# A planned one-core encoder layer: listed times of loads and small steps, and where a gate's tile is loaded

## The chip, the cores and the metric

The kernel runs on one core of one Trainium2 chip. The metric is the device time of one execution in microseconds, as the median of several; a shorter time is better. The engines are named as the profile names them: PE (TensorE), ACT (ScalarE), DVE (VectorE), POOL (GpSimd) and SP (SyncE, whose queue issues nearly all DMAs).

## The reference

One layer over a sequence of 2048 tokens of width 1024, in float32. Two mixers read the same normalised input: banded attention over chunks of 64 tokens (8 heads) and an mLSTM, a matrix memory carried from chunk to chunk (4 heads). Their gated sum is projected and added, and a feed-forward part of width 4096 follows.

```python
xn = rms_norm(x, mix_norm_g)
aq, ak, av, mq, mk, mv, mo, ipre, fpre, ga, gm = split(xn @ w_in)
att = chunk_band_attention(aq, ak, av, rel_bias)
hm = mlstm_chunkwise(*silu(conv(mq, mk)), mv, ipre + b_igate, fpre + b_fgate)
mlstm_out = sigmoid(mo) * rms_norm(hm, mh_norm_g)          # per head; the output gate
y = sigmoid(ga) * (att @ w_att_proj) + sigmoid(gm) * (mlstm_out @ w_mlstm_proj)
x = x + y @ w_out
x = x + square(relu(rms_norm(x, ffn_norm_g) @ w_up)) @ w_down
return rms_norm(x, final_norm_g)
```

## The kernel before

The 2048 tokens are four blocks of 512 (b = 0 to 3), handled as two halves of two. Every dense product is computed with operands split into two parts of reduced precision, so that each product is three matmuls of 512 columns (`mm3`, `quad`, `product`, `down`), and the large products are cut by Strassen's scheme into seven sub-products, m = 0 to 6. What such a sub-product needs on the activations' side (a sum of blocks, split in two) is an operand; a weight tile is loaded into `wraw` and split into `wsp` (ACT L483, DVE L485).

The first pass over the input projection serves blocks 0 and 1 (`quad`), the second pass serves blocks 2 and 3 (`in_far`), in three batches of sub-products, (0, 3, 1), (2, 4) and (5, 6). The second pass's operands are computed early and kept in device memory as `xu`. `take_batch` loads them into a ring of 16 tiles: for each m and k it waits for the tile to be kept and for a free ring slot, and spawns `take_u1`, which loads (L2055) and splits the tile (a cast on ACT, L1061, and a subtraction on DVE, L1066). Four loads serve one m.

The mixers of blocks 0 and 1 run beside the second pass, those of blocks 2 and 3 beside the first half's downward product. They consist of many small steps. For attention, `scores` multiplies (L1289), finds maxima (DVE, L1295), takes exponentials (ACT, L1302) and normalises on ACT or DVE (L1309, L1307), `turn` transposes (L1321) and splits (L1324, L1326), and `weigh` multiplies by the values (L1214), which were loaded from `vspill` (L1093). For the mLSTM, `gates_rest` computes a block's gate sums in some sixty steps on tiles of 16 columns, and `rec_head` computes one head of one block: it waits for its loads (`load_rec`), weighs the scores in tile `w`, multiplies `w` by the values for each of four chunks (L1564) with the carried state (L1568, L1572), collects the outputs (`rec_out`), normalises them in eight steps on tiles of 4 columns, transposes them (L1603), and multiplies them by the output gate (L1605), which it loads from `mfar` into a tile of the pool `temp` (L1599). One head is worked on at a time (`rec_room`).

At the start `norm_in(b)` sums the squares of blocks 0 and 1 (L977), takes the inverse root on POOL (L981, L985), and `rows_far` spreads it over the partitions with PE (L1020).

The order of the work comes from a planner, `Flow`. Each part is a generator; it yields the engine that it needs and how long it takes there in ns (and, as a third number, how long its result takes to land after that), or it waits for an event or a free tile. The planner keeps a clock for each engine and always lists the request that could start first. The instructions come out in that order, and a scheduler behind it lists each engine's own queue, in which ACT's and DVE's instructions may be pulled ahead by up to 6 and 10 us of planner's time. A load is planned like this:

```python
yield "sp", 800, 2000            # SP for 800 ns; landed 2000 ns later
self.nc.sync.dma_start(r[:, 1].bitcast(F32), src)
yield from self.split(r[:, 1].bitcast(F32), r)
```

So the numbers in the yields move instructions within the queues; they do not change what the chip does with one. Each engine works its queue off in order, and an instruction whose input is late holds what stands behind it.

Of the kernel before, what the change touches and what calls it, by code (L numbers as in the profile page):

```python
# [36 lines left out]
MH = 4  # L37
# [65 lines left out]
class Flow:  # L103
# [11 lines left out]
               dve=dict(pe=220.0, act=130.0, dve=130.0, pool=155.0), pool=dict(pe=290.0, act=130.0, dve=60.0),  # L115
# [119 lines left out]
def dve_ns(n):  # L235
    return 70 + 1.042 * n
# [12 lines left out]
class Layer:  # L249
# [710 lines left out]
    def norm_in(self, b):  # L960
        fl, nc = self.fl, self.nc
        B = self.blk[b]
        r, ev = self.rin[b], [Event() for _ in range(KT)]
        (slot,) = yield "get", self.sc, 1
        tot = slot[0]
        B["xg"] = yield "get", self.rpool, KT
        fl.set(B["xg_ev"])
        if b == 1:
            yield "wait", self.w_sent
        for k in range(KT):  # L970
            (x,) = yield "get", self.ctx, 1
            fl.spawn(self.square_in(b, k, x, tot, ev), b)
        yield "wait", ev
        (bk,) = yield "get", self.banks, 1
        yield "pe~", 900
        for t in range(NT):
            nc.tensor.matmul(bk[:, 2 * t:2 * t + 2], tot[:, t * P:(t + 1) * P], self.ones,  # L977
                             start=True, stop=True)
        fl.put(self.sc, slot)
        yield "dve", 75  # L980
        nc.vector.tensor_scalar(r, bk[:, :2 * NT].rearrange("p (t a) -> p t a", a=2)[:, :, 0], 1.0 / D, EPS,  # L981
                                op0=ALU.mult, op1=ALU.add)
        fl.put(self.banks, bk)
        yield "pool", 3600
        nc.gpsimd.tensor_tensor(r, r, self.half, op=ALU.pow)  # L985
        fl.set(self.ev_r[b])
    def stats_far(self):
# [396 lines left out]
    def gates_rest(self, b, bk):  # L1384
# [10 lines left out]
        yield "dve", 85  # L1395
        V.tensor_scalar(d, e, 2.0, None, op0=ALU.add)
        yield "dve", 85
        V.reciprocal(d, d)
        yield "dve", 85
        V.tensor_mul(s, e, d)  # L1400
        yield "dve", 85
        V.tensor_mul(s2, s, s)
        yield "dve", 85
        V.tensor_scalar(p, s2, 1.0 / 15, None, op0=ALU.mult)
        for m in (13, 11, 9, 7, 5, 3):
            yield "dve", 85
            V.scalar_tensor_tensor(p, p, 1.0 / m, s2, op0=ALU.add, op1=ALU.mult)
        yield "dve", 85
        V.scalar_tensor_tensor(p, p, 1.0, s, op0=ALU.add, op1=ALU.mult)
        yield "dve", 85  # L1410
        V.tensor_scalar(v4("lf"), fg, 0.0, None, op0=ALU.min)
        yield "dve", 85
        V.scalar_tensor_tensor(sm["lf"], p, -2.0, sm["lf"], op0=ALU.mult, op1=ALU.add)
        yield "pe~", 300
        nc.tensor.matmul(bk[:, 0:16], self.tri, sm["lf"], start=True, stop=True)
        nc.tensor.matmul(bk[:, 16:32], self.ones[:, 0:1].to_broadcast([P, P]), sm["lf"], start=True, stop=True)
        yield "dve", 85
        V.tensor_copy(sm["bc"], bk[:, 0:16])
        yield "dve", 85
        V.tensor_copy(sm["bl"], bk[:, 16:32])  # L1420
        yield "dve", 85
# [4 lines left out]
        yield "dve", 85  # L1426
        V.tensor_copy(a[:, 64:], bk[:16, 128:256])
        sh = 1
        while sh < P:
# [9 lines left out]
        yield "dve", 85  # L1439
        V.tensor_copy(sm["um"], bk[:, 272:288])  # L1440
        ms, ml, bl = self.ms, v4("ml"), v4("bl")
        if b > 0:
            yield "dve", 85
            V.tensor_copy(ms[:, 0], ms[:, NT])
        for c in range(NT):
            yield "dve", 85
            V.tensor_tensor(ml[:, c], ms[:, c], um[:, c], op=ALU.max)
            yield "dve", 85
            V.tensor_add(ms[:, c + 1], ml[:, c], bl[:, c])
        msf = ms.rearrange("p a b -> p (a b)")[:, :16]  # L1450
        yield "dve", 85
        V.tensor_tensor(sm["mt"], msf, bk[:, 256:272], op=ALU.max)
        ex = self.ex
        yield "dve", 85
        V.scalar_tensor_tensor(ex[:, 0], sm["mt"], -1.0, sm["bc"], op0=ALU.mult, op1=ALU.subtract)
        yield "dve", 85
        V.tensor_sub(ex[:, 1], msf, sm["mt"])
        yield "dve", 85
        V.tensor_sub(ex[:, 2], sm["u"], sm["ml"])
        yield "dve", 85  # L1460
        V.tensor_sub(ex[:, 3], msf, sm["ml"])
        yield "act", 150
        nc.scalar.activation(ex, ex, AF.Exp)
        yield "dve", 85
        V.tensor_scalar(ex[:, 1], ex[:, 1], 0.5, None, op0=ALU.mult)
        yield "dve", 85
# [55 lines left out]
    def rec_head(self, b, h, r):  # L1522
# [53 lines left out]
        yield "dve", 85  # L1576
        V.scalar_tensor_tensor(hs[:, 0], den, -1.0, den, op0=ALU.mult, op1=ALU.max)
        yield "dve", 85
        V.tensor_tensor(hs[:, 0], hs[:, 0], exh, op=ALU.max)
        yield "dve", 85  # L1580
        V.reciprocal(hs[:, 0], hs[:, 0])
        yield "dve", 85
        V.tensor_mul(hs[:, 1], hs[:, 0], hs[:, 0])
        yield "dve", 85
        V.tensor_mul(hs[:, 1], hs[:, 1], hs[:, 2])
        yield "dve", 85
# [3 lines left out]
        yield "dve", 85  # L1590
        V.tensor_mul(hs[:, 0], hs[:, 0], hs[:, 1])
        yield "dve", dve_ns(512)
        V.tensor_mul(ndv[:, :, :128], ndv[:, :, :128],
                     hs[:, 0].rearrange("p (c o) -> p c o", o=1).to_broadcast([P, NT, P]))
        fl.put(self.hs, hs)
        (og,) = yield "get", self.temp, 1
        yield "wait", [self.m_ev[b, 2 * MH + h]]
        yield "sp", 800, 2000
        nc.sync.dma_start(og[:, :512], self.mfar[b].ap()[2 * MH + h])  # L1599
        (bk,) = yield "get", self.banks, 1  # L1600
        yield "pe~", 107 * NT
        for c in range(NT):
            nc.tensor.transpose(bk[:, c * P:(c + 1) * P], ndv[:, c, :128], self.ident)  # L1603
        yield "dve", dve_ns(512)
        V.tensor_mul(kt[:, :512], bk, og[:, :512])  # L1605
# [10 lines left out]
        fl.put(self.rpool, r)  # L1616
        fl.put(self.rec_room, 0)
        fl.set(B["rec_ev"][h])

    def rec_out(self, n, bk, nd, hs, c, ev, old):  # L1620
        fl, nc = self.fl, self.nc
# [428 lines left out]
        yield "wait", aev[ORDER[-1], 3]  # L2050
        fl.put(self.rpool, *(yield "get", ring, N_RING[s]))

    def take_u1(self, src, r, ev):
        yield "sp", 800, 2000
        self.nc.sync.dma_start(r[:, 1].bitcast(F32), src)  # L2055
        yield from self.split(r[:, 1].bitcast(F32), r)
        self.fl.set(ev)
# [279 lines left out]
    def build(self):  # L2337
# [37 lines left out]
        for b in range(NB):  # L2375
            self.blk.append(dict(
                xg=[], xg_ev=Event(), xn=E(KT), x2=E(KT), kq_all=Event(), begun=Event(), opened=Event(), how={}, mix_got=Event(), head_done=E(AH), gates=Event(), ctx={},
                qk_ev=E(2 * MH), mix=[None] * 8, mix_ev=E(8), mixed=E(8), mix_left=[4] * 4 + [1] * 4, rec_ev=E(MH),
                mid=Event(), vo={}, vn={}, vp_ev=E(4), mvh_ev=E(MH), row_ev=E(MH), rows=Event(), gf=Event(), heads_left=[2] * 4))
        fl.spawn(self.setup(), 0)  # L2380
        fl.spawn(self.norm_in(0), 0)
# [103 lines left out]
```

## Time and profile before

| | us |
|---|---|
| median of 3 runs (lowest to highest) | 2751.83 (2751.77 to 2754.45) |
| the profiled execution | 2750.82 |
| its span, first to last instruction | 2749.0 |
| PE busy | 2725.4 |
| DVE busy | 2085.9 |
| ACT busy | 1527.8 |
| POOL busy | 44.0 |
| DMA, mean rate | 245 GB/s |

The profile comes from one execution. Busy times add up the instructions of an engine; PE's matmuls overlap one another, so PE counts as busy where they follow each other without a hole. The granted clock of PE is 0.998 of full speed over the whole span.

### The profile page before, as it was taken

To read this page: it belongs to the slowest core of one execution; us is meant where nothing else is said; L and a number is where in the kernel's file an instruction comes from. 1 tells how busy PE (TensorE), PEld (TensorE's weight loads), DVE (VectorE), ACT (ScalarE), POOL (GpSimd) and SP (SyncE) were. 2 spreads that over 40 slices of the span, in tenths; PEclk is the share of its full clock that TensorE was granted. 3 is DMA by queue.
4 is the path that set the end of the run, shared out by engine and by line. 5 is a ranking of instruction groups with operands and counts; after the bars stand their busy time and mean duration, and the time that the engine had idled before them with its cause. 6 is when DMAs were issued, how large, how long until landed. Compare 5 with 4: busy or idle time off the path is not lost.

```text
span 2749.0 us, 38064 instructions
## 1 busy us (share of the span) xinstructions
PE 2725.4 (99%) x12840; PEld 2263.1 (82%) x12840; DVE 2085.9 (76%) x3686; ACT 1527.8 (56%) x2635; POOL 44.0 (2%) x76
## 2 busy tenths in 40 slices
PE   9999999999999999999999999999999999999998
PEld 7878888788888888888888888888888888888887
DVE  7868776888775778897668899888788665667675
ACT  6545446666652434566556766656345565564443
POOL 0000000000000000000000000000000000000000
PEclk9999999999999999999999999999999999999999
DMA  8877678778777898767668777786774454578763
GB/s 286 288 257 262 240 264 280 254 238 269 251 256 254 299 319 289 250 212 262 247 235 296 254 239 227 240 254 203 279 239 164 154 202 158 187 272 283 273 233 126
DMA packets 330840, 673.05 MB, mean 245 GB/s; under 512 B 36772, under 2 KB 66852, under 8 KB 330644
## 3 DMA queue, kind: packets, MB, share of 16 engines
q1 hardware_dynamic: 330500, 670.60, 72.5%
q8 instruction: 101, 1.65, 0.2%
q14 instruction: 95, 0.78, 0.1%
q10 hardware_dynamic: 144, 0.01, 0.0%
HBM read 458.27 MB, written 212.21 MB: 244 GB/s over the span
## 4 chain that ended last, share of the span: by engine, by line
PE 86%; DVE 6%; issue 3%; DMA 2%; ACT 2%; POOL 0%; SPq 0%; POOLq 0%; ACTq 0%; DVEq 0%
PE bank L613 36%; PE bank L644 12%; PE bank L545 9%; PE bank L544 9%; PE bank L546 9%; PE bank L649 2%; PE bank L1289 2%; PE bank L1214 2%; PE bank L1321 2%; DVE wsp L485 1%; DVE r L1066 1%; PE bank L1372 1%; PE bank L1564 0%; DVE sc L1295 0%; DVE ctx L1717 0%
## 5 line engine op out<-in xcount | busy, mean ns | idle before, releaser
L613 PE MATMUL bank<-r,wsp 128*128 128x512 f32 x4872 | 1111.1, 390 | 2.6 <-DVE r L1066 0.7
L613 PEld LDWEIGHTS bank<-r,wsp 128*128 128x128 f32 x4872 | 912.2, 188 | 197.0 <-DVE ctx L1750 2.0
L483 ACT CAST wsp<-wraw 128x1024 fp32r<-128x1024 f32 x439 | 461.1, 1050 | 460.5 <-PE bank L613 182.6
L485 DVE TENSOR_TENSOR wsp<-wraw,wsp 128x1024 fp32r<-128x1024 f32 x439 | 536.4, 1222 | 231.9 <-ACT wsp L483 228.7
L544 PE MATMUL bank<-r,wsp 128*128 128x512 f32 x1152 | 455.0, 395 | 0.3 <-DVE scs L1295 0.3
L546 PE MATMUL bank<-r,wsp 128*128 128x512 f32 x1152 | 450.2, 391 | 0.0
L545 PE MATMUL bank<-r,wsp 128*128 128x512 f32 x1152 | 450.1, 391 | 0.0
L644 PE MATMUL bank<-r,wsp 128*128 128x512 f32 x1512 | 370.1, 394 | 0.7 <-ACT r L1324 0.6
L644 PEld LDWEIGHTS bank<-r,wsp 128*128 128x128 f32 x1512 | 279.4, 188 | 56.5 <-ACT r L1324 0.8
L546 PEld LDWEIGHTS bank<-r,wsp 128*128 128x128 f32 x1152 | 216.3, 188 | 45.5
L544 PEld LDWEIGHTS bank<-r,wsp 128*128 128x128 f32 x1152 | 216.5, 188 | 41.0 <-DVE scs L1295 0.7
L545 PEld LDWEIGHTS bank<-r,wsp 128*128 128x128 f32 x1152 | 216.7, 188 | 40.4
L1066 DVE TENSOR_TENSOR r<-r 128x512 fp32r<-128x512 f32 x273 | 181.9, 686 | 70.5 <-ACT r L1061 69.2
L1061 ACT CAST r<-r 128x512 fp32r<-128x512 f32 x273 | 165.1, 620 | 126.1 <-DMA r<-u 101.3
L1750 DVE TENSOR_TENSOR ctx<-bank,ctx 128x512 f32<-128x512 f32 x150 | 102.7, 686 | 64.1 <-PE bank L613 63.0
L502 DVE TENSOR_TENSOR wraw<-wraw,wraw 128x1024 f32<-128x1024 f32 x112 | 136.3, 1218 | 1.9 <-DMA wsum<-wraw 0.7
L1302 ACT ACTIVATE sc<-sc,scs 128x640 f32<-128x640 f32 (+4 forms) x128 | 97.3, 761 | 54.0 <-DVE scs L1295 53.4
L1742 ACT COPY ctx<-bank 128x512 f32<-128x512 f32 x150 | 87.2, 581 | 52.4 <-PE bank L613 51.5
L2071 ACT ACTIVATE ctx<-ctx 128x512 f32<-128x512 f32 x96 | 60.5, 630 | 99.2 <-DVE ctx L1750 99.1
L1326 DVE TENSOR_TENSOR r<-bank,r 128x512 fp32r<-128x512 f32 (+1 forms) x168 | 96.4, 594 | 8.8 <-ACT r L1324 8.0
L1214 PE MATMUL bank<-r,r 128*128 128x512 f32 x336 | 95.8, 367 | 3.3 <-DVE ctx L1626 2.9
L1324 ACT CAST r<-bank 128x512 fp32r<-128x512 f32 (+1 forms) x168 | 80.8, 514 | 27.7 <-PE bank L1321 27.2
(246 smaller groups left out, 2975.3 us busy)
## 6 DMA issues: line engine op xcount, KB each, us to landing
wraw<-in_wf SPq DMA_DIRECT2D x196, 512.0 KB, 4.2
wraw<-wsum SPq DMA_DIRECT2D x112, 512.0 KB, 5.1
r<-u SPq DMA_DIRECT2D x224, 256.0 KB, 4.8
u<-ctx SPq DMA_DIRECT2D x128, 256.0 KB, 2.8
u<-tmp SPq DMA_DIRECT2D x96, 256.0 KB, 2.1
wraw<-in_w SPq DMA_DIRECT2D x47, 512.0 KB, 3.8
ctx<-in_wf SPq DMA_DIRECT2D x88, 256.0 KB, 4.2
wsum<-ctx SPq DMA_DIRECT2D x88, 256.0 KB, 2.9
```

What stands on the lines that cost most here:

```text
L483: nc.scalar.copy(w[:, 0], raw)
L485: nc.vector.tensor_sub(w[:, 1], raw, w[:, 0].bitcast(F32))
L502: V.tensor_sub(dst, x, y)
L544: mm(ps, lh, rh, start=first, stop=False)
L545: mm(ps, lh, rl, start=False, stop=False)
L546: mm(ps, ll, rh, start=False, stop=last)
L613: mm(ps, wv[:, x, k, n], a[:, y], start=new and k == 0 and x == y == 0, stop=k == 3 and x == 1, skip_group_check=True)
L644: mm(ps, wv[:, x, k, n], a[:, y], start=start and x == y == 0, stop=stop and x == 1, skip_group_check=True)
L1061: self.nc.scalar.copy(dst[:, 0], src)
L1066: self.nc.vector.tensor_sub(dst[:, 1], src, dst[:, 0].bitcast(F32))
L1214: nc.tensor.matmul(bkv[:, :, c0:c0 + w], st, sl[:, :, o:o + w], start=n == 0, stop=n == total - 1)
L1750: nc.vector.tensor_add(t[:, o:o + 512], ps, t[:, o:o + 512])
```

## The change

Four edits, all in what the planner is told or where a tile is kept.

1. `take_batch` tells the planner that a load of the second pass's operands lands 4500 ns after its issue; 2000 before. The other users of `take_u1` keep 2000.
2. `norm_in` tells it that the inverse root on POOL lands 3000 ns after its 3600 in the case b = 0; for b = 1 nothing is added.
3. In `rec_head` the output gate's tile is loaded into `w`, the tile of the weighted scores, which nobody reads after the last chunk's product. The load is a generator of its own, `load_gate`, spawned when the last chunk's product is listed, before the wait for the outputs. Before, a `temp` tile was taken and the load was listed after the normalisation. The multiplication waits for the new event `og_ev`.
4. The small DVE steps of `gates_rest` and `rec_head` are planned with 150 ns each instead of 85.

```diff
@@ take_batch
-                fl.spawn(self.take_u1(self.xud.ap()[m, k], r, aev[m][k]), 0)
+                fl.spawn(self.take_u1(self.xud.ap()[m, k], r, aev[m][k], 4500), 0)
@@ norm_in
-        yield "pool", 3600
+        yield "pool", 3600, 0 if b else 3000
@@ gates_rest, 25 places (some in loops), and rec_head, 7 places
-        yield "dve", 85
+        yield "dve", 150
...
@@ rec_head
+        fl.spawn(self.load_gate(b, h, w), 1)
         yield "wait", nev
...
         fl.put(self.hs, hs)
-        (og,) = yield "get", self.temp, 1
-        yield "wait", [self.m_ev[b, 2 * MH + h]]
-        yield "sp", 800, 2000
-        nc.sync.dma_start(og[:, :512], self.mfar[b].ap()[2 * MH + h])
         (bk,) = yield "get", self.banks, 1
         yield "pe~", 107 * NT
         for c in range(NT):
             nc.tensor.transpose(bk[:, c * P:(c + 1) * P], ndv[:, c, :128], self.ident)
+        yield "wait", [B["og_ev"][h]]
         yield "dve", dve_ns(512)
-        V.tensor_mul(kt[:, :512], bk, og[:, :512])
+        V.tensor_mul(kt[:, :512], bk, w[:, :512])
         fl.put(self.banks, bk)
-        fl.put(self.temp, og)
...
+    def load_gate(self, b, h, w):
+        yield "wait", [self.m_ev[b, 2 * MH + h]]
+        yield "sp", 800, 2000
+        self.nc.sync.dma_start(w[:, :512], self.mfar[b].ap()[2 * MH + h])
+        self.fl.set(self.blk[b]["og_ev"][h])
@@ take_u1
-    def take_u1(self, src, r, ev):
-        yield "sp", 800, 2000
+    def take_u1(self, src, r, ev, landing=2000):
+        yield "sp", 800, landing
```

More of the change, by code (lines that the diff above doesn't have):

```diff
@@ L1394, in gates_rest @@
         e, d, s, s2, p = (sm[n] for n in ("e", "d", "s", "s2", "p"))
-        yield "dve", 85
+        yield "dve", 150
         V.tensor_scalar(d, e, 2.0, None, op0=ALU.add)
-        yield "dve", 85
+        yield "dve", 150
         V.reciprocal(d, d)
-        yield "dve", 85
+        yield "dve", 150
         V.tensor_mul(s, e, d)
-        yield "dve", 85
+        yield "dve", 150
         V.tensor_mul(s2, s, s)
-        yield "dve", 85
+        yield "dve", 150
         V.tensor_scalar(p, s2, 1.0 / 15, None, op0=ALU.mult)
         for m in (13, 11, 9, 7, 5, 3):
-            yield "dve", 85
+            yield "dve", 150
             V.scalar_tensor_tensor(p, p, 1.0 / m, s2, op0=ALU.add, op1=ALU.mult)
-        yield "dve", 85
+        yield "dve", 150
         V.scalar_tensor_tensor(p, p, 1.0, s, op0=ALU.add, op1=ALU.mult)
-        yield "dve", 85
+        yield "dve", 150
         V.tensor_scalar(v4("lf"), fg, 0.0, None, op0=ALU.min)
-        yield "dve", 85
+        yield "dve", 150
         V.scalar_tensor_tensor(sm["lf"], p, -2.0, sm["lf"], op0=ALU.mult, op1=ALU.add)
@@ L1416, in gates_rest @@
         nc.tensor.matmul(bk[:, 16:32], self.ones[:, 0:1].to_broadcast([P, P]), sm["lf"], start=True, stop=True)
-        yield "dve", 85
+        yield "dve", 150
         V.tensor_copy(sm["bc"], bk[:, 0:16])
-        yield "dve", 85
+        yield "dve", 150
         V.tensor_copy(sm["bl"], bk[:, 16:32])
-        yield "dve", 85
+        yield "dve", 150
         V.tensor_sub(v4("u"), ig, v4("bc"))
@@ L1442, in gates_rest @@
         if b > 0:
-            yield "dve", 85
+            yield "dve", 150
             V.tensor_copy(ms[:, 0], ms[:, NT])
         for c in range(NT):
-            yield "dve", 85
+            yield "dve", 150
             V.tensor_tensor(ml[:, c], ms[:, c], um[:, c], op=ALU.max)
-            yield "dve", 85
+            yield "dve", 150
             V.tensor_add(ms[:, c + 1], ml[:, c], bl[:, c])
         msf = ms.rearrange("p a b -> p (a b)")[:, :16]
-        yield "dve", 85
+        yield "dve", 150
         V.tensor_tensor(sm["mt"], msf, bk[:, 256:272], op=ALU.max)
         ex = self.ex
-        yield "dve", 85
+        yield "dve", 150
         V.scalar_tensor_tensor(ex[:, 0], sm["mt"], -1.0, sm["bc"], op0=ALU.mult, op1=ALU.subtract)
-        yield "dve", 85
+        yield "dve", 150
         V.tensor_sub(ex[:, 1], msf, sm["mt"])
-        yield "dve", 85
+        yield "dve", 150
         V.tensor_sub(ex[:, 2], sm["u"], sm["ml"])
-        yield "dve", 85
+        yield "dve", 150
         V.tensor_sub(ex[:, 3], msf, sm["ml"])
@@ L1575, in rec_head @@
         exh = ex[:, 0].rearrange("p (c m) -> p c m", c=NT)[:, :, h]
-        yield "dve", 85
+        yield "dve", 150
         V.scalar_tensor_tensor(hs[:, 0], den, -1.0, den, op0=ALU.mult, op1=ALU.max)
-        yield "dve", 85
+        yield "dve", 150
         V.tensor_tensor(hs[:, 0], hs[:, 0], exh, op=ALU.max)
-        yield "dve", 85
+        yield "dve", 150
         V.reciprocal(hs[:, 0], hs[:, 0])
-        yield "dve", 85
+        yield "dve", 150
         V.tensor_mul(hs[:, 1], hs[:, 0], hs[:, 0])
-        yield "dve", 85
+        yield "dve", 150
         V.tensor_mul(hs[:, 1], hs[:, 1], hs[:, 2])
-        yield "dve", 85
+        yield "dve", 150
         V.tensor_scalar(hs[:, 1], hs[:, 1], 1.0 / P, EPS, op0=ALU.mult, op1=ALU.add)
```

12 lines of the change are left out of this document (6 added, 6 removed).

## The prediction, made before the changed kernel was run

> **What bounds the kernel now.** I read the page's first part, then the windows by stage, then PE's waits, then the timeline at the longest wait.
>
> ```profile
> span 2749.0 us, 38064 instructions
> ...
> PE 2725.4 (99%) x12840; PEld 2263.1 (82%) x12840; DVE 2085.9 (76%) x3686; ACT 1527.8 (56%) x2635; POOL 44.0 (2%) x76
> ```
>
> PE is busy in 2725.4 of 2749.0 us, so only what is not matmul work can be won: 23.6 us of idle time and what slow stretches of PE hide. The windows say where it lies (span and PE busy are the first two numbers, the granted clock is the third from the end).
>
> ```profile
> 450.00:750.00 300.00, 293.91 (x1603) 248.35 (x1602) 239.78 (x664) 201.05 (x468) 13.01 (x25) 1.00 0.82 259
> ...
> 1450.00:1950.00 500.00, 496.99 (x2610) 419.49 (x2609) 430.08 (x1031) 329.75 (x675) 17.86 (x32) 1.00 0.78 248
> 1950.00:2700.00 750.00, 748.97 (x3319) 620.02 (x3318) 528.58 (x686) 390.46 (x569) 2.94 (x2) 1.00 0.63 219
> 2700.00:2749.00 49.00, 40.45 (x211) 34.26 (x210) 20.44 (x29) 13.67 (x20) 2.01 (x2) 0.96 0.26 97
> ```
>
> The stage in which the first two blocks' mixers run beside dense products (450 to 750) idles 6.1 us, the same stage for blocks 2 and 3 (1450 to 1950) 3.0 us, the end (from 2700) 8.6 us, and the 750 us between hardly 1. The rest, some 5 us, is the start and 750 to 1450. Built, the changed kernel has the same 12,514 matmuls, and the first 135 and the last 3543 of them stand in the old order. So the end and the second downward product stay as they are, and everything is decided between 30 us and about 1940 us: 14 us of idle time at most.
>
> ```profile
> PE bank L1214 <- DVE ctx L1626: 2.9, 1, 2.9
> PE bank L1321 <- ACT sc L1309: 1.6, 3, 0.8
> PE bank L1020 <- POOL r_in L985: 1.0, 1, 1.0
> ...
> PE bank L1415 <- DVE g_lf L1413: 0.9, 1, 0.9
> ```
>
> PE's longest waits are one of 2.9 us and a few of about 1. The page's chain of waits gives PE 86% of the span, which says the same.
>
> **Edit 1: the second pass's loads (take_batch, L2055).** This is what the 2.9 us are:
>
> ```profile
> 739.91 0.60 PE L1321 MATMUL bank<-const,sc 128*128 128x128 f32 x4
> 740.00 4.53 SPq L2055 DMA_DIRECT2D r<-xu  x4
> ...
> 740.82 1.56 PE L644 MATMUL bank<-r,wsp 128*128 128x512 f32 x6
> ...
> 746.57 0.62 ACT L1061 CAST r<-r 128x512 fp32r<-128x512 f32 x1 [5.43 <-DMA r<-xu]
> ...
> 747.22 0.69 DVE L1066 TENSOR_TENSOR r<-r 128x512 fp32r<-128x512 f32 x1 [3.79 <-ACT r L1061]
> ...
> 747.83 0.29 DVE L1626 TENSOR_TENSOR ctx<-bank,ctx 128x129 f32<-128x129 f32 x1
> ...
> 748.17 1.22 PE L1214 MATMUL bank<-r,r 128*128 128x512 f32 x2 [2.87 <-DVE ctx L1626]
> ...
> 749.19 2.61 PE L644 MATMUL bank<-r,wsp 128*128 128x512 f32 x6
> ```
>
> Four loads of xu are issued from 740.00 on. The first lands 6.5 us later; the cast L1061, which stands early in ACT's list, holds ACT for 5.43 us; behind it wait DVE's L1066 and L1626; and L1214 on PE starts late by 2.87 us. PE then runs slowly: six L644 take 2.61 us instead of 1.56 and the two L1214 1.22 instead of some 0.66 (two of such six), 1.6 us more. The wait costs 4.5 us in all.
>
> Does the new landing, 4500 instead of 2000, remove it? In a built order I count the matmuls listed between two instructions and price them by these rows:
>
> ```profile
> 2250.00:2300.00 50.00, 50.00 (x222) 41.38 (x222) 26.74 (x30) 26.04 (x39) 0.00 (x0) 1.00 0.39 142
> ```
>
> ```profile
> L1321 PE MATMUL bank<-const,sc 128*128 128x128 f32 x560 | 82.1, 275 | 2.7 <-ACT sc L1309 1.6 <-DVE sc L1307 0.7 <-DVE scs L1295 0.3
> ```
>
> A 512-column matmul costs 50.00/222 = 0.225 us, a 128-column one 0.109 ((0.60 - 0.275)/3 from the four L1321 at 739.91), others in proportion. Before, the cast stands 2.5 us of PE work behind its load (8 of 512 columns and 5 short ones) and the first PE instruction that hangs on it 2.6 us further: 5.1 us of cover against 6.5 of landing plus 1.6 from cast to PE, which gives 3.0, the measured wait. In the changed order the cast of this first load stands 2.5 us behind it again: the scheduler that lists the instructions last pulled it forward. But the first PE instruction behind it (an L1321 whose bank an L1295 must free) is now 4.6 us further (12 of 512 columns, 12 of 128, 4 others). Cover 7.1 us; from cast to PE 0.62 + 0.69 + about 0.8 for the two reads of L1295 = 2.1.
>
> ```profile
> r<-xu SPq DMA_DIRECT2D x28, 256.0 KB, 4.6
> ...
> r<-vspill SPq DMA_DIRECT2D x28, 512.0 KB, 6.5
> ...
> tmp<-mfar SPq DMA_DIRECT2D x16, 256.0 KB, 4.4
> ```
>
> With the 4.6 us median landing of xu, 6.7 us, nothing is left to wait; with 6.5 us, 1.6 are. I take none: **-4.5 us** (bounds -4.5 and, with 1.6 of idle and a slow clock again, -1.3). Of the other 27 xu loads, 16 keep their distance; for three the cast moves 1.7 to 2.0 us further behind, for the last eight up to 3.6 us, these in a stage that hardly idles: nothing.
>
> The Trainium skill (DMA: Bandwidth & Descriptors, "Anatomy of one DMA — SWDGE (gpsimd) path") fits 2.0 us plus bytes over 436 GB/s, for another queue kind; as an estimate that is 2.6 us for 256 KB. By it the old 2000 would be nearly right and the new 4500 an error; the 4.6 us row and the 5.43 us of idle ACT contradict it here.
>
> **The slow clock.** It decides what a new wait costs.
>
> ```profile
> 32.00:36.00 4.00, 4.00 (x15) 3.37 (x15) 4.00 (x10) 3.93 (x9) 0.00 (x0) 0.66 0.97 268
> ...
> 744.00:752.00 8.00, 5.13 (x22) 4.12 (x21) 4.24 (x8) 5.35 (x12) 0.00 (x0) 0.79 0.46 165
> ...
> 1710.00:1714.00 4.00, 3.58 (x18) 3.06 (x19) 3.89 (x14) 4.00 (x9) 0.00 (x0) 1.00 0.98 266
> ```
>
> The granted clock was 0.79 over the 8 us that hold the 2.87 us wait, and 0.66 after the idle 0.98 us at 31 us (quoted below); after the 0.9 us wait of L1415 at 1710 it stayed 1.00. So I charge 1.6 us to any idle time of about 1 us or more, and nothing below. The Trainium skill (TensorE: Matmul & The Clock Gate, "Why this matters for your kernels") allows idle gaps up to about 3 us; by that no wait here would slow PE, and the slower rival below would come to 4.9 us instead of 6.5, under the bound of 0.2%, which would move its share to "same". The row of 0.66 after 0.98 us of idle time speaks against it.
>
> **Edit 2: 3000 ns behind the pow of norm_in (L985).** The 3000 apply to block 0 alone; what moves is block 1.
>
> ```profile
> 29.59 1.46 POOL L985 TENSOR_TENSOR r_in<-r_in,half 128x4 f32<-128x4 f32 x1 [29.15 <-DVE r_in L981]
> ...
> 31.10 1.93 PE L1020 MATMUL bank<-const,r_in 128*128 128x128 f32 x8 [0.98 <-POOL r_in L985]
> ```
>
> ```profile
> 49.17 0.95 PE L977 MATMUL bank<-ones,sc 128*128 128x2 f32 x8
> ...
> 50.16 0.16 DVE L981 TENSOR_SCALAR r_in<-bank 128x4 f32<-128x4 f32 x1 [1.96 <-PE bank L977]
> ...
> 50.40 1.01 POOL L985 TENSOR_TENSOR r_in<-r_in,half 128x4 f32<-128x4 f32 x1 [19.35 <-DVE r_in L981]
> ...
> 52.35 1.05 PE L1020 MATMUL bank<-const,r_in 128*128 128x128 f32 x8
> ```
>
> In block 0 L1020 waits 0.98 us for this pow, and the changed order keeps L1020's place, three matmuls behind L977: nothing gained there. In block 1 the trace shows no wait, since ten matmuls stand between L977 and L1020. The changed order leaves two there. L977 ends at 50.12; the pow ends at 51.41 and L1020 can start at 51.46; the two matmuls, 0.45 us, would let it start at 50.57. **+0.9 us**, with PE idle about 0.7, under the point where the clock falls. Bounds: 0.7 and 2.5 (with the clock).
>
> **Edit 3: the gate's tile (load_gate, rec_head).** 16 loads of mfar go into w, spawned as soon as the last scores product is listed, before the wait for the four outputs. Sixteen gets and puts of temp go. Each store or load around is the same work on SP's queue.
>
> ```profile
> L1921 DVE SCALAR_TENSOR_TENSOR ctx<-ctx,ctx 128x512 f32<-128x512 f32 x32 | 21.8, 684 | 0.9 <-ACT ctx L1919 0.6
> ...
> L1605 DVE TENSOR_TENSOR ctx<-bank,tmp 128x512 f32<-128x512 f32 x16 | 10.9, 684 | 1.0 <-PE bank L1603 1.0
> ...
> L1579 DVE TENSOR_TENSOR hs<-hs,g_ex 128x4 f32<-128x4 f32 x16 | 2.9, 181 | 0.3
> ```
>
> ```profile
> DMA to landing us min/median/max: 3.0/4.4/6.8
> ```
>
> L1605, which multiplies by the gate, idled 1.0 us before, all of it for PE: no gate was ever late, so an earlier load wins nothing by itself. In the changed order 15 of 16 gates have 5.9 us or more from the place where SP can issue them to their use. Head 1 of block 0 does not: its load stands behind a wsum store that waits for DVE's L427, 2.5 us before L1605, which stands 0.45 us before the L1289 whose bank it frees. SP can run 0.7 us ahead of the list there, so landing + 0.69 + 0.2 stands against 3.7: 1.6 us late with the 4.4 us median, 0.2 with 3.0. **+0.5**, nearer to the trace, in which this never cost (bounds 0 and 4.0, with 6.8 of landing).
>
> **Edit 4: small steps at 150 instead of 85.** L1579's 181 ns says 150 is the truer price. No instruction is added; the edit moves the list. What it may win is in the short waits: the two mixer stages idle 9.1 us, 6.2 without the xu wait. The PE instructions listed less than 1.2 us behind the ACT or DVE instruction that they wait for are 163 before and 169 after. Hence I take **0**, bounds -4 and +4. Block 2's and 3's recurrences end some 40 us earlier in the list; the projection that waits for them stands where it stood, so that is no gain. Six normalisations of scores move from DVE to ACT, and four quarter tiles are split in place instead of stored (four stores of 64 KB and one load fewer): both beside a PE that is busy.
>
> **What the new order brings unasked.** The load of r<-vspill for block 1's first pair of heads (block 0's half) now stands behind an mfar store that waits for DVE's L1921, 3.5 us of PE work before the L1214 that reads it (12 of 512 columns and 5 shorter); before, the shortest such distance was 6.8. L1921 is listed 5.7 us ahead of that L1214; with its 684 ns and some 0.6 for the store's issue and the signals, SP cannot send the load earlier than 4.4 us ahead.
>
> ```profile
> DMA to landing us min/median/max: 4.5/6.5/8.1
> ```
>
> Landing in 6.5 us it is 2.1 late, and the clock follows: **+3.7 us** (bounds: 0.1 with 4.5 of landing, 3.7 + 1.6 = 5.3 with 8.1).
>
> **Sum.** -4.5 + 0.9 + 0.5 + 0 + 3.7 = **+0.6 us**. The profiled execution took 2750.82 us (span 2749.0 and 1.8 around it), 1.0 below the median of 2751.83; so 2751.4 there and **2752.4** as a median. I call 0.2% or 5.5 us what a measurement of this kernel can tell from no change.
>
> **Rivals.** *The vspill load is in time* (it lands in 4.5, or SP runs further ahead): -4.5 + 0.9 + 0.5 = -3.1, 2748.7. For it: the list of PE's waits names no DMA. Against: no vspill load stood so close.
>
> *Faster: the short waits go too.* If the truer prices keep DVE's small steps from crowding the evacuations, half of the 6.2 us goes on top: -3.1 - 3.1 = -6.2, 2745.6. For it: 181 ns were listed as 85. Against: 163 and 169 close pairs.
>
> *Slower: transfers land at the long end.* Place: the mixer stage of blocks 0 and 1, where DMA is busy 0.82 of the time. xu at 6.5 us gives back all but 1.3; vspill at 8.1 costs 5.3; the gate 1.6 and the pow 0.9: +6.5, 2758.3. It is slower than before from a vspill landing of about 5 us on if xu also lands late, and by over 5.5 us from about 7.2. *The edit doesn't do what it says* is part of it: the cast that was to be moved stands 2.5 us behind its load as before, and only other work ahead of the wait saves it.
>
> **Numbers.** Forecast 0.47, vspill in time 0.25, short waits go 0.12, long landings 0.16. Each carries some 4 us of unread reshuffling. Faster by over 0.2% (under 2746.3): most of the third, a fifth of the second, a little of the first: 0.18. Slower (over 2757.3): most of the fourth and a tenth of the first: 0.18. Same 0.64. The range 2745.6 to 2758.3 runs from the one outer rival to the other.
>
> **What would show it.** Right: no 2.9 us wait of an L1214 on L1626 near 745, and PE's granted clock 1.00 there; an L1214 that waits 1 to 4 us for a DMA near 595 us, with L644 at 0.43 us apart behind it; an L1020 wait of about 0.7 us near 51; L1020's 0.98 at 31 unchanged; the windows from 1950 on unchanged to 0.3 us. Wrong: xu's cast still ending a wait of PE, a summed idle time of the two mixer stages that differs from 9.1 us by over 5, or any difference after 1950.

## The result, and the profile after

The changed kernel took 2762.86 us (median of 6, 2761.06 to 2764.45), the kernel before beside it on the same chip 2751.8 (6 runs, 2750.82 to 2755.3). The medians differ by 11.1 us. The ratio, which is used from here on, is 1.0034, with a 95% interval of 1.0024 to 1.0045: 9.4 us slower (6.6 to 12.4). The forecast was 2752.4 with a range up to 2758.3; it was wrong. Left out of the ratios below are three single executions (of the kernel before, of edit 2 and of the scores' chain) that took over 1.5% longer than the fastest of their kernel.

The windows of the kernel after, by stage (span, PE's busy time, then the other engines, the granted clock third from the end):

```profile
0.00:450.00 450.00, 446.33 (x1997) 366.56 (x1998) 344.52 (x535) 245.30 (x380) 6.20 (x12) 1.00 0.77 268
450.00:750.00 300.00, 291.42 (x1605) 246.05 (x1604) 239.94 (x678) 206.76 (x484) 13.96 (x27) 1.00 0.83 257
750.00:1450.00 700.00, 695.62 (x3095) 572.45 (x3094) 517.91 (x724) 343.53 (x509) 1.01 (x1) 1.00 0.76 260
1450.00:1950.00 500.00, 492.71 (x2572) 414.64 (x2570) 422.48 (x1022) 329.44 (x679) 18.35 (x32) 0.99 0.76 241
1950.00:2700.00 750.00, 749.59 (x3322) 620.87 (x3323) 531.06 (x689) 390.40 (x568) 2.94 (x2) 1.00 0.65 222
```

PE's work is what it was (2726.2 us busy after, 2725.4 before), and the span grew by 10.3 us. Idle time, span less PE's busy time: the first two blocks' mixers 8.6 us (6.1 before), 750 to 1450 4.4 (1.3 before), the last two blocks' mixers 7.3 (3.0 before), and 0.4 from 1950 to 2700 (1.0 before). So in this pair of executions the loss lies where the mixers run, and between them. One execution shows this only roughly. The runs of edit 2, of edit 1 for batch (5, 6), of xu at 2050 and of xu for sub-product 4 (4500 and 6500), all described below, have PE's old order in these stages, or nearly. The windows of 1450 to 1950 in the run of edit 2 and in that of sub-product 4 at 4500:

```profile
1450.00:1950.00 500.00, 494.41 (x2595) 416.57 (x2594) 428.55 (x1029) 327.66 (x672) 18.45 (x32) 1.00 0.78 246
```

```profile
1450.00:1950.00 500.00, 493.20 (x2587) 414.82 (x2586) 428.37 (x1030) 328.23 (x674) 18.91 (x32) 1.00 0.78 245
```

They idle 5.6 and 6.8 us there, with the order that idled 3.0 in the profile before. From 750 to 1450 the five idle 3.4 to 4.1 us, so the 4.4 of the changed kernel is hardly a loss. In the two mixer stages together the old order idles 8.4 to 12.7 us in these five and the profile before, the changed kernel 15.9: the loss shows in the mixer stages, and how it is split between them one execution does not tell.

PE's waits in the kernel after (summed us, times, the longest):

```profile
PE bank L1321 <- ACT sc L1309: 2.8, 5, 1.2
PE bank L644 <- DVE ctx L762: 2.4, 3, 1.4
PE bank L1538 <- DMA r<-mfar: 2.4, 2, 1.8
PE bank L1020 <- POOL r_in L985: 2.1, 2, 1.1
PE bank L1600 <- DVE ctx L1594: 2.1, 3, 0.8
PE bank L1289 <- DVE scs L1295: 1.9, 2, 1.0
```

The one long wait of before (2.9 us, L1214 for L1626) is gone. These six rows hold seventeen waits, none over 1.8 us; in the kernel before, the first four rows of the same view held six. The worst place is this, PE's timeline and the windows over it:

```profile
1526.69 0.39 PE L546 MATMUL bank<-r,wsp 128*128 128x512 f32 x1
1526.92 0.51 PE L1289 MATMUL bank<-r,r 128*128 128x384 f32 x2
1528.26 1.22 PE L1289 MATMUL bank<-r,r 128*128 128x384 f32 x4 [0.83 <-DVE scs L1295]
1530.52 1.01 PE L1289 MATMUL bank<-r,r 128*128 128x384 f32 x2 [1.05 <-DVE scs L1295]
1531.33 0.84 PE L1321 MATMUL bank<-const,sc 128*128 128x128 f32 x3
1533.34 1.76 PE L1321 MATMUL bank<-const,sc 128*128 128x128 f32 x7 [1.17 <-ACT sc L1309]
1534.75 0.78 PE L544 MATMUL bank<-r,wsp 128*128 128x512 f32 x1
```

```profile
1528.00:1532.00 4.00, 2.69 (x9) 1.75 (x9) 2.78 (x10) 2.94 (x6) 0.11 (x1) 0.81 0.95 333
1532.00:1536.00 4.00, 2.83 (x11) 2.47 (x11) 3.50 (x9) 4.00 (x8) 0.63 (x1) 0.50 0.94 308
1536.00:1540.00 4.00, 4.00 (x16) 3.20 (x16) 3.96 (x10) 2.95 (x8) 0.20 (x1) 0.84 0.78 306
```

From 1526.9 to 1534.7 no dense matmul is listed. PE has only scores (L1289) and their transposes (L1321), each of which waits for its DVE or ACT step; three waits of about 1 us add up to 3.05, and the clock falls to 0.50. In the kernel before, the profile names no wait of PE between 1500 and 1540 us: groups of L544 to L546 stand between most of these steps there. Some of its rows (of the dense groups from 1517.47 to 1519.63 and from 1520.23 to 1521.69 only the first row is shown):

```profile
1516.52 0.75 PE L1289 MATMUL bank<-r,r 128*128 128x256 f32 x4
1517.11 0.60 PE L1321 MATMUL bank<-const,sc 128*128 128x128 f32 x4
1517.47 0.48 PE L544 MATMUL bank<-r,wsp 128*128 128x512 f32 x1
...
1519.63 0.84 PE L1321 MATMUL bank<-const,sc 128*128 128x128 f32 x6
1520.23 0.48 PE L544 MATMUL bank<-r,wsp 128*128 128x512 f32 x1
...
1521.69 0.75 PE L1289 MATMUL bank<-r,r 128*128 128x256 f32 x4
```

### The profile page after: what moved, and what is told of

It reads as the page before. It is cut to its first block, busy times and chain, and to the rows that moved or that the text cites. A ratio compares the mean times of both kernels' runs of the same rounds, so it can differ in the third digit from the quotient of the medians.

```text
span 2759.3 us, 38042 instructions
## 1 busy us (share of the span) xinstructions
PE 2726.2 (99%) x12840; PEld 2263.2 (82%) x12840; DVE 2083.5 (76%) x3683; ACT 1534.3 (56%) x2644; POOL 44.5 (2%) x76
## 5 line engine op out<-in xcount | busy, mean ns | idle before, releaser
L544 PE MATMUL bank<-r,wsp 128*128 128x512 f32 x1152 | 456.4, 397 | 0.0
L546 PE MATMUL bank<-r,wsp 128*128 128x512 f32 x1152 | 450.4, 391 | 0.0
L546 PEld LDWEIGHTS bank<-r,wsp 128*128 128x128 f32 x1152 | 216.5, 188 | 45.9
L544 PEld LDWEIGHTS bank<-r,wsp 128*128 128x128 f32 x1152 | 216.8, 188 | 41.1 <-DVE r L1326 0.4
L1214 PE MATMUL bank<-r,r 128*128 128x512 f32 x336 | 95.1, 364 | 0.6 <-DVE r L1326 0.5
```

The source lines that it names most:

```text
L544: mm(ps, lh, rh, start=first, stop=False)
L546: mm(ps, ll, rh, start=False, stop=last)
```

## The experiments

All run times stand against the kernel before, run beside them on the same chip. In the ratios a thousandth is 2.75 us. For each kernel I also compare the built order of PE's some 12,500 matmuls, by their lines in the program, with that of before and count the places at which the two differ. A matmul that moves counts up to twice, where it stood and where it stands now, so about half as many matmuls move as there are places.

### Each edit alone

Edit 1 alone:

```diff
-                fl.spawn(self.take_u1(self.xud.ap()[m, k], r, aev[m][k]), 0)
+                fl.spawn(self.take_u1(self.xud.ap()[m, k], r, aev[m][k], 4500), 0)
```

> Edit 1 alone on the kernel before (xu loads listed with 4500 ns of landing). Every theory has the 2.87 us wait of L1214 for DVE's L1626 near 748 us gone. Theory A (edit 4 carries the loss) and theory C (edit 3 does): 4.5 us less than the kernel before, and no other window worse by more than 1 us. Theory B (any edit re-lists the mixers and scatters short waits, and the terms do not add): the 4.5 us come, but idle time elsewhere between 450 and 1950 us moves by 2 us or more, to either side.

Measured: 1.0011 (1.0001 to 1.0021), +3.0 us. Stretches of 450 to 790 us, first of before, then of this run, and this run's waits there:

```profile
450.00:550.00 100.00, 97.68 (x526) 80.95 (x525) 74.06 (x207) 67.79 (x169) 3.97 (x9) 1.00 0.86 266
550.00:650.00 100.00, 99.13 (x537) 83.53 (x537) 83.22 (x250) 65.30 (x149) 4.33 (x8) 1.00 0.81 252
650.00:740.00 90.00, 89.97 (x507) 77.81 (x506) 78.09 (x199) 63.99 (x142) 4.07 (x7) 1.00 0.82 265
740.00:790.00 50.00, 47.13 (x241) 39.86 (x240) 37.65 (x82) 32.08 (x66) 1.71 (x3) 0.97 0.71 238
```

```profile
450.00:550.00 100.00, 94.75 (x519) 78.29 (x519) 70.93 (x202) 67.05 (x168) 4.09 (x8) 1.00 0.90 261
550.00:650.00 100.00, 98.21 (x532) 81.98 (x531) 85.01 (x257) 71.15 (x161) 5.00 (x9) 1.00 0.83 247
650.00:740.00 90.00, 87.80 (x495) 75.30 (x494) 76.88 (x193) 62.53 (x136) 4.78 (x8) 1.00 0.82 256
740.00:790.00 50.00, 50.00 (x263) 42.69 (x262) 37.22 (x80) 34.19 (x70) 1.11 (x2) 1.00 0.81 270
```

```profile
PE bank L1538 <- DMA r<-mfar: 3.2, 2, 2.3
PE bank L1321 <- ACT sc L1309: 3.1, 3, 1.7
PE bank L1321 <- DVE scs L1295: 1.4, 2, 1.1
```

The edit does what it says where it was aimed: 2.87 us of idle time from 740 to 790 become 0. But the order differs in 2,236 places between about 470 and 810 us, and from 450 to 740 the idle time goes from 3.2 to 9.2 us, for loads of mfar and for steps of the scores, which do not read xu. Six other executions with the old order up to 740 us idle 3.7 to 5.9 there, so the 9.2 lies outside that scatter. That is theory B's picture.

Edit 2 alone:

```diff
-        yield "pool", 3600
+        yield "pool", 3600, 0 if b else 3000
```

> Edit 2 alone (3000 ns behind block 0's pow). Theories A and C: +0.9 us, a wait of L1020 for POOL's L985 near 50 us of about 1 us, and nothing else. Theory B: besides it the idle time between 450 and 1950 us moves by 2 us or more although edit 2 stands 400 us ahead of it.

Measured: 1.0004 (0.9993 to 1.0014), +1.1 us. Only 18 places differ, all before 55 us, so theory B's "listed anew" was no possibility here. The idle time between 450 and 1950 us moved all the same, from 10.4 to 15.7 us, by over the 2 us that theory B had named: with the same order this is scatter between executions, and it says how little one profile's idle time can carry. The new wait is there, 1.15 us in this run and in the kernel after, whose row this is:

```profile
50.12 1.16 PE L1020 MATMUL bank<-const,r_in 128*128 128x128 f32 x8 [1.15 <-POOL r_in L985]
```

Edit 3 alone (the diff of `rec_head` and `load_gate` above):

> Edit 3 alone (the gate loaded into the weighted scores' tile). Theory C (gate loads go ahead of the mfar loads that L1538 reads): 3 to 8 us slower, L1538 waits for r<-mfar as after the change (2.4 us in 2 waits). Theory A: within 1.5 us of the kernel before. Theory B: several us to either side, out of waits of mixed kinds.

Measured: 1.0002 (0.9991 to 1.0013), +0.6 us, with 4,398 places that differ. Theory C falls: the waits for r<-mfar add up to 0.2 us, and in no profile with this edit did anything wait for a gate's load.

Edit 4 alone (the 32 small steps at 150):

> Edit 4 alone (32 small steps listed at 150 ns). Theory A: 9 to 14 us slower (what the change lost, plus what edit 1 won), with the stall at about 1528 us where L1289 waits for its evacuations L1295 and L1321 for L1309. Theory C: within 2 us of the kernel before. Theory B: several us to either side, but the four runs do not add up to the 11.1 us of the whole change to within 3 us.

Measured: 1.0023 (1.0013 to 1.0032), +6.3 us, the largest of the four: less than theory A's 9 to 14, and not within theory C's 2. It has the stall of the kernel after, its first two waits to 0.01 us (shown are the rows with a wait):

```profile
1522.84 1.22 PE L1289 MATMUL bank<-r,r 128*128 128x384 f32 x4 [0.83 <-DVE scs L1295]
...
1525.10 0.62 PE L1289 MATMUL bank<-r,r 128*128 128x384 f32 x2 [1.05 <-DVE scs L1295]
...
1527.92 0.98 PE L1321 MATMUL bank<-const,sc 128*128 128x128 f32 x7 [1.87 <-ACT sc L1309]
```

The four make +11.0 us together, the whole change +9.4. So they add, against my expectation under theory B, but with intervals of some 3 us on each the sum could not have told much.

### Is it the price, or any new listing?

The price of the 32 steps at 90, 120 and 180:

```diff
-        yield "dve", 85
+        yield "dve", 90      # 120, 180
```

> The 32 small steps at 90 ns instead of 85, nothing else: a price that means nothing, but the listing of the mixers moves. Theory A (the price itself costs: the higher it is, the worse the mixers are listed; 150 measured +6 us): +0.5 us. Theory B (the listing of before is one draw among many, and lies at the low end; any nudge draws anew): somewhere from 0 to +8 us, as likely +5 as 150 was.

> The 32 small steps at 120 ns. Theory A: +3 us, between 90 and 150. Theory B: 0 to +8 us, in no order with 90, 150 and 180.

> The 32 small steps at 180 ns, what the reciprocals and the 128x4 steps take on the chip. Theory A: +9 us. Theory B: 0 to +8 us, in no order with the others. A third theory, that a truer price is better and 150 only fell short of it: back to 0 or below.

Measured: 90: 1.0046 (1.0030 to 1.0061), +12.7 us. 120: 1.0010 (0.9999 to 1.0020), +2.8. 180: 1.0030 (1.0018 to 1.0042), +8.3. Five ns per step cost more than 95. Theory A, in which the loss grows with the price, falls, and so does the third, that a truer price is better. The 12.7 lies above theory B's 0 to 8 as well.

And below 85:

> The 32 small steps at 80 ns, 5 less than before. Theory A2 (more than 85 is bad for the mixers, whatever the size: 90, 120, 150 and 180 measured +12.7, +2.8, +6.3 and +8.3 us): 0 or a little below. Theory B (each listing is a draw, and that of before is a low one): +2 to +10 us as the others.

> The 32 small steps at 60 ns. Theory A2: 0 or below. Theory B: +2 to +10 us, in no order with 80.

Measured: 80: 1.0005 (0.9996 to 1.0014), +1.4. 60: 1.0012 (1.0003 to 1.0021), +3.3. The 80 is less than theory B's +2 to +10, and its interval holds 0, which A2 allows; the interval of the 60 (0.8 to 5.8 us) lies above 0, against A2.

Edit 1 with 50 ns instead of 2500 added:

```diff
-                fl.spawn(self.take_u1(self.xud.ap()[m, k], r, aev[m][k]), 0)
+                fl.spawn(self.take_u1(self.xud.ap()[m, k], r, aev[m][k], 2050), 0)
```

> Edit 1 with 2050 ns of landing instead of 4500: 50 ns that mean nothing. Theory A: 0, the 2.87 us wait of L1214 for L1626 near 748 us stays. Theory B: the listing behind about 400 us is drawn anew, 0 to +8 us; the 2.87 us wait may be gone or not.

Measured: 0.9999 (0.9990 to 1.0007). I had expected a wide redraw; only 174 places differ, all between about 750 and 815 us. The wait of L1214 is there with 1.41 us. So the run tells for neither theory, but gives a point with few places changed.

The changed kernel with the small steps back at 85:

> The changed kernel with the small steps back at 85 (edits 1 to 3). If the edits' measured shares add (+3.0, +1.1 and +0.6): +4.7 us over the kernel before, 5 below the changed one, and no stall of some 6 us near 1528 us. The prediction's sum for the three, without its vspill wait: -3.1. Theory B: anything from 0 to +10.

Measured: 1.0024 (1.0015 to 1.0033), +6.6 us; the shares of the three edits make 4.7, the prediction's terms without vspill -3.1. The stall near 1528 is gone: no wait over 0.2 us between 1500 and 1560. Yet this execution idles 7.5 us from 1450 to 1950, as the kernel after does, with other waits (it took 2766.30 us, the longest of its eleven, so part of that can be scatter). So the stall comes with edit 4; the kernel without it is 2.8 us better by the ratios, and the intervals, some 3 us to either side of each, do not tell this from the 5 us of the sum.

Edit 4 for blocks 2 and 3 alone:

```diff
-        yield "dve", 85
+        yield "dve", 150 if b > 1 else 85
```

> The kernel before with edit 4 for blocks 2 and 3 alone: the order is the one of before up to about 1450 us, drawn anew from there. Theory B: the idle time up to 1450 us stays as before (11 us), that of 1450 to 1950 rises from 3.0 to the 5 to 12 that it had in the other listings: +2 to +6 us. Theory A (the steps' price acts on the first two blocks' recurrences, which are the ones under pressure): 0.

Measured: 1.0027 (1.0016 to 1.0037), +7.4 us, with 2,785 places that differ, all behind about 1450 us. The stall is the same:

```profile
1528.54 1.21 PE L1289 MATMUL bank<-r,r 128*128 128x384 f32 x4 [0.83 <-DVE scs L1295]
...
1530.81 0.62 PE L1289 MATMUL bank<-r,r 128*128 128x384 f32 x2 [1.06 <-DVE scs L1295]
...
1533.63 1.75 PE L1321 MATMUL bank<-const,sc 128*128 128x128 f32 x7 [1.87 <-ACT sc L1309]
```

So all of edit 4's loss can come from one stage listed anew, that of blocks 2 and 3. Theory A, which put it in blocks 0 and 1 and had 0 here, falls; whether those add a few us, the intervals do not tell.

### Do truer prices mend it?

load_rec's loads at what they take:

```diff
-            yield "sp", 800, 2000
+            yield "sp", 800, 4500      # in three places
```

> The changed kernel with load_rec's loads (the row, k and q, the values) listed with 4500 ns of landing, what they take on the chip, in place of 2000. Every theory: no wait of L1538 or L1549 for r<-mfar (2.6 us in the changed kernel) and of L1289 behind it. If these waits carry the loss: 3 to 5 us below the changed kernel. Theory B: a new draw, so the sum of PE's idle time between 450 and 1950 us moves by several us for other waits than these, to either side.

Measured: 1.0057 (1.0043 to 1.0070), +15.7 us, 6 worse than the kernel after. The waits for r<-mfar fall from 2.6 us to one of 0.5, nearly as every theory had it; the loss did not go with them. The stall near 1528 is there too, with the same three waits.

The scores' chain at what it takes, on the kernel after and on the kernel before:

```diff
-            yield "dve", dve_ns(w)                      # L1295
+            yield "dve", dve_ns(w) + 200
-        yield "act", act_ns(n, ap=2)                    # L1302
+        yield "act", act_ns(n, ap=2) + 180
-        yield "dve", 75                                 # L1304
+        yield "dve", 160
-        e0 = yield "act|dve", 60 + dve2_ns(n)           # L1309, L1307
+        e0 = yield "act|dve", 200 + dve2_ns(n)
```

> The changed kernel with the scores' chain listed at what it takes on the chip (L1295 200 ns longer, L1302 180, L1304 160 in place of 75, L1309 and L1307 140 longer). Theory D (the waits come where that chain is listed too short: L1321 for L1309 is the largest wait of most listings, 2.8 us in the changed kernel): this wait and L1289's for L1295 fall below 1 us together, 4 to 7 us less than the changed kernel. Theory B: these waits get smaller, others come, the sum stays within 4 us of the changed kernel.

> The kernel before with the scores' chain listed at what it takes, as in the run above. Theory D: 1 to 3 us less than before (its waits of L1321 for L1309 and L1307 were 2.3 us). Theory B: a new draw, 0 to +8 us.

Measured: 1.0076 (1.0061 to 1.0091), +20.9 us, on the kernel after; 1.0040 (1.0025 to 1.0055), +11.0 us, on the kernel before. Theory D falls clearly, and both are beyond theory B's bounds too (within 4 us of the kernel after, and 0 to 8). The waits it was aimed at stay (L1321 for L1309 2.0 and L1289 for L1295 2.9 us in the first, L1321 for L1309 3.9 us in one piece in the second), and the mixers run on past 1950, where the kernel before idles 1.0 us. The windows of the two:

```profile
1950.00:2700.00 750.00, 741.31 (x3288) 611.85 (x3288) 529.70 (x714) 397.21 (x590) 2.93 (x2) 0.99 0.62 213
```

```profile
1950.00:2700.00 750.00, 742.48 (x3288) 614.11 (x3287) 527.26 (x706) 392.71 (x580) 3.94 (x3) 0.99 0.63 215
```

8.7 and 7.5 us idle. The last L1214 starts at 1982 and 1978 us there, at 1931 in the kernel before. Told that its steps take longer, the planner spreads the mixers over more time.

### What is edit 1's own worth?

> The kernel before with edit 1 for the last batch of sub-products (5, 6) alone, whose loads made the 2.87 us wait near 748 us. This leaves PE's order as it was, all but some 100 instructions that change a bank or swap by a place; ACT's and DVE's queues move around those loads. Theory B (edit 1 is right, the listing it draws anew gave its gain back): the wait is gone, 3 to 4.5 us less than the kernel before, idle time elsewhere as before. Rival (edit 1's gain was never there, since xu's landing only moves the wait): 0, with another wait near 748 us.

Measured: 0.9998 (0.9990 to 1.0007). A miss of mine: batch (5, 6) is not the one. The four loads issued at 740 belong to sub-product 4, and PE's order is the one of before to the last matmul. It is of use all the same: it shows how the same order scatters. The wait was 1.55 us in this execution (2.00 and 1.46 in those of edit 2 and of edit 4 for blocks 2 and 3, whose order is the old one here too), and the clock stayed at 1.00 around it in all three; and from 750 to 1450 it idled 3.6 us where the profile before shows 1.3. The wait's row and that window:

```profile
746.25 0.73 PE L1214 MATMUL bank<-r,r 128*128 128x512 f32 x2 [1.55 <-DVE ctx L1626]
```

```profile
750.00:1450.00 700.00, 696.38 (x3103) 572.45 (x3102) 522.02 (x745) 347.20 (x524) 2.08 (x3) 1.00 0.77 260
```

Then the right loads:

```diff
-                fl.spawn(self.take_u1(self.xud.ap()[m, k], r, aev[m][k]), 0)
+                fl.spawn(self.take_u1(self.xud.ap()[m, k], r, aev[m][k], 4500 if m == 4 else 2000), 0)   # and 6500
```

> The run before this one told the longer landing to loads that stand after the wait, so it says nothing of edit 1. Here the four loads that made the 2.87 us wait near 748 us (those of sub-product 4, issued at 740) are told 4500, the rest stays: the kernel before with 108 of PE's 12516 matmuls in other places, all between about 680 and 790 us, and the cast of xu behind the work that fed L1214. Theory B (edit 1's reason is right, its other 2100 moved matmuls gave the gain back): no wait of L1214 for L1626, granted clock 1.00 from 744 to 752, 3 to 4.5 us less than the kernel before. Rival (the cast only blocks something else): a wait of 1 us or more within 10 us of the place, 0 in all.

> The same with 6500 ns, what the first of these loads took: 38 matmuls in other places. Theory B: 3 to 4.5 us less, as with 4500. Rival: 0. A difference of over 2 us between the two would say that even so short a stretch drawn anew counts.

Measured: 4500: 0.9991 (0.9981 to 1.0000), -2.5 us. 6500: 0.9995 (0.9984 to 1.0006), -1.4. The window over the place, first of the 4500, then of the 6500:

```profile
744.00:752.00 8.00, 8.00 (x50) 7.05 (x50) 5.27 (x11) 5.49 (x13) 0.64 (x1) 1.00 0.83 279
```

```profile
744.00:752.00 8.00, 8.00 (x49) 7.12 (x48) 7.41 (x18) 6.89 (x19) 0.00 (x0) 1.00 0.69 228
```

The wait is gone in both and nothing near takes its place, so the other wait that the rival had is not there. Edit 1's reason holds; its worth is measured as 2.5 and 1.4 us, less than the 3 to 4.5 that I expected and about the wait of 1.5 to 2.0 us that other executions of the old order have at this place. The first interval ends at 0 and the second holds it, so the gain itself is not clear of noise. (The places that differ lie between about 750 and 815 us, not 680 and 790 as I wrote.) These two are the best of all that ran: not to be told from the kernel before, and by the ratios 11 to 12 us under the changed kernel.

### All listings together

| kernel | places that differ | against before, us |
|---|---|---|
| edit 1 for batch (5, 6) | 0 | -0.6 |
| edit 2 | 18 | +1.1 |
| xu of sub-product 4 at 6500 | 38 | -1.4 |
| xu of sub-product 4 at 4500 | 108 | -2.5 |
| xu at 2050 | 174 | -0.3 |
| edit 1 | 2,236 | +3.0 |
| edit 4, blocks 2 and 3 | 2,785 | +7.4 |
| small steps at 80 | 2,932 | +1.4 |
| edits 1 to 3 | 4,253 | +6.6 |
| edit 3 | 4,398 | +0.6 |
| small steps at 60 | 4,565 | +3.3 |
| edit 4 (150) | 4,644 | +6.3 |
| small steps at 120 | 4,698 | +2.8 |
| scores' chain | 4,886 | +11.0 |
| small steps at 90 | 5,181 | +12.7 |
| changed kernel and scores' chain | 5,334 | +20.9 |
| changed kernel and load_rec at 4500 | 5,389 | +15.7 |
| changed kernel | 5,569 | +9.4 |
| small steps at 180 | 5,887 | +8.3 |

Below 200 places five kernels lie from -2.5 to +1.1, and no interval among them lies clear of 0. Above 2,000 all fourteen are at or above the kernel before, by 0.6 to 20.9, whatever was told, more or less, truer or not; three of them (+0.6, +1.4 and +2.8) are not clear of 0, and several share edits. The size does not go by the count: edit 3 has 4,398 places and +0.6, the 90 has 5,181 and +12.7. In the two mixer stages together the fourteen idle 10.6 to 18.9 us, twelve of them over 13, where executions of the old order idle 8.4 to 12.7. What is shown: the loss comes with the mixers being listed anew. What stays open is why none of the fourteen came out better. That the old order is a low one among the many that the planner can give fits; but most of those that were told longer times (90, 150, 180, load_rec, the chain) lost more than those told shorter ones (60, 80), though 120 did not, and I have not told these two apart.

## Why the prediction was wrong

**The step that failed** is "Edit 4: ... Hence I take 0, bounds -4 and +4", and with it the "some 4 us of unread reshuffling" that each case carried. Edit 4 alone measured +6.3 us (3.6 to 8.8), and the rest of what edit 1 moves cost some 4.4 to 5.5 more (+3.0 alone, less -1.4 or -2.5, each with an interval of some 3 us to either side). The 163 close pairs before and 169 after did not show it: they count pairs one by one, and the stall near 1528 is eight L1289 and ten L1321 in one row with no dense matmul between them to cover their waits, which the old order has nowhere. And I centred the term at 0 with both signs alike, where fourteen listings gave no gain.

**Edit 1, -4.5.** The mechanism was right (no wait at 748, 8.00 of 8.00 us busy from 744 to 752 in the kernel after and in both runs for sub-product 4), the size was not. Apart from the rest it is worth 2.5 us (0 to 5.2) and 1.4 (-1.7 to 4.4). The profile before had caught a long landing with a slow clock, 2.87 + 1.6; other executions of that order wait 1.5 to 2.0 us at a full clock. And alone the edit cost 3.0.

**Edit 2, +0.9.** Right in its mechanism; the +1.1 measured has an interval from -1.9 to 3.9 and does not test the size by itself. The wait of block 1's L1020 was 1.15 us (0.7 expected; the pow took 1.4 us instead of 1.0), L1020's 0.98 at 31 us was unchanged, and the clock did not fall (1.00 over 48 to 54).

**Edit 3, +0.5.** +0.6 measured, but not as worked out: the gate's loads landed in 3.1 us at the median, and nobody waited for one. The agreement is luck, within an interval of -2.5 to 3.6.

**The vspill load, +3.7.** It did not come. The load was issued at 589.47 and read at 594.40, 4.9 us ahead where I had taken 4.4 at most, and these loads landed in 4.7 us at the median after against 6.5 before. So the first rival (vspill in time) was right in its place.

**The rivals.** "Slower: transfers land at the long end" named the right sign and the wrong cause: xu, vspill and gate were all in time. The transfers that were late, 2.4 us of r<-mfar before L1538, I had not looked at. Such waits of over 2 us stand in the profiles of edit 1 (3.2), of edit 4 (2.5, before L1289) and of the small steps at 90 (2.4), and there is none in that of edits 1 to 3 together: they come with the listing, not with one edit.

**What would show it.** The two mixer stages' idle time was to differ from 9.1 us by no more than 5; it is 15.9, which said "wrong". "Unchanged to 0.3 us" from 1950 on did not quite hold: 0.4 us idle against 1.0, a difference for the better and within the 0.1 to 1.0 of other executions of the old order.

**Time by the median.** The forecast stood on one execution of 2750.82 us. Later runs of the same kernel, on five chips, have medians of 2753.65 to 2755.81 (21 to 35 runs) and spread over 2750 to 2765; the profile before showed an execution near the lower end, with 1.3 us idle from 750 to 1450 and 3.0 from 1450 to 1950, where the same order idled 3.4 to 4.1 and 3.3 to 6.8 in other executions. So part of the 9.1 us that the signs were measured against was the luck of one execution.

## What to carry to other kernels

Where a planner lists the work, a number told to it has two effects: the instruction that it was meant for, and the listing of everything behind it. The first can be read from the trace (edits 1 and 2 here); the second was larger. So before pricing such an edit, count how much of the built order moves: with fewer than 200 differing places the edits stayed within 2.5 us of the kernel before, with more than 2,000 the new listing decided, and in these fourteen never to the better. Hence tell the planner the new number at the one place where the trace shows the wait (four loads of 28 here), and keep the rest of the order; here that took the wait away, for a gain at the edge of what could be measured.

## What the runs showed of the hardware

A wait of 0.98 us did not slow PE as a rule, as I had taken it to. L1020's wait at 30.8 us is in every profile; over 32 to 36 us the granted clock was 0.65 to 0.72 in four of twenty executions (0.66 in the kernel before) and 1.00 in the other sixteen, among them the kernel after:

```profile
32.00:36.00 4.00, 4.00 (x19) 3.31 (x18) 4.00 (x9) 4.00 (x10) 0.00 (x0) 1.00 0.89 271
```

Nor did one of 1.55 us at 746, shown above. Yet in the kernel after three waits of 0.83 to 1.17 us within 6 us, at 1528, left 0.50. The same stall left 0.59 and 0.56 in the run of edit 4 for blocks 2 and 3, and a full clock in that of edit 4 alone, where the waits add up to 3.75 us; this is the window behind them:

```profile
1528.00:1532.00 4.00, 4.00 (x21) 3.10 (x22) 3.82 (x8) 4.00 (x9) 0.63 (x1) 1.00 0.99 364
```

So neither a single wait nor such a row of waits slows PE each time, and what decides it is open. The Trainium skill (TensorE: Matmul & The Clock Gate, "Why this matters for your kernels") holds idle gaps up to some 3 us harmless; sixteen of twenty executions agree with it at the first place, four do not. The loads of one line, L2058, landed in 2.6 to 9.7 us within the kernel after's one execution (median 4.5). That may be one reason why one and the same order scatters by several us; no run here tests it.
